# Keeping the residual by tokens, and writing the first FFN product of a transformer layer as seven block products

## The chip, the cores and the metric

The kernel runs on one core of a Trainium2 chip. The metric is the time of one execution in microseconds (us) on the device.

## The reference, cut to what matters

One layer with S = 512 tokens, D = 1024 features, an FFN width of 2816 and a side input p of width 256, all in float32:

```python
merged = sigmoid(gate_a) * (y_nsa @ w_up_nsa) + sigmoid(gate_b) * (y_moba @ w_up_moba)
x = x + merged @ w_out
gate, up = split(rms_norm(x, g_ffn) @ w_ffn_in, 2, axis=-1)
x = x + (silu(gate) * up) @ w_ffn_out
ple_gate = sigmoid(rms_norm(x, g_ple) @ w_ple_gate)
x = x + ple_gate * (p @ w_ple_proj)
```

`y_nsa` and `y_moba` come from two attention mixers (compressed, selected and windowed heads; block-selected heads), which the change leaves as they are.

## The kernel before, in words

**Precision and weights.** Each float32 matrix is split into a high half of reduced width and a low rest, and each product is three matmuls (high by high, high by low, low by high; helper `tmm`, L370 to L375). The class `Weights` (L57 to L104) keeps a list of units in the order of use. SyncE loads a unit of 128 x 1024 (512 KB) into `wr` (3 buffers), ScalarE copies the high half (`wh`, L87), VectorE subtracts the low half (`wl`, L88), 4 buffers each. `get` splits two units ahead and loads six ahead. The statements are put into each engine's order by the framework's scheduler, which reorders the program; each engine then works its own list in order and waits on semaphores.

**Stages.** Input projections and rotary embedding (0 to 160 us), attention (160 to 378) with the gate and up products woven in, the second up product, the output projection, the first FFN product (448 to 678), the second (678 to 788), the side input and its gate.

**Weight sums.** The second FFN product is done by blocks: the matrix is cut in 2 x 2 blocks, and seven half-size products replace eight (L1048 to L1089), four of them with sums of weight blocks. Those sums (`fs1` to `fs4`) are made in DRAM by `weight_sums` (L911 to L923): 32 transfers of 704 KB on GpSimd's software queue, 16 plain copies and 16 that accumulate, each issued after a mark that GpSimd copies once per attention step.

**Output projection** (L950 to L974). The residual `X2` is kept by features: eight tiles of 128 features x 512 tokens, from `xT`. Per tile, 24 matmuls with the weight stationary and 512 tokens moving; then `residual` adds the projection to `X2` on VectorE, `norm_split` writes the two halves of the tile times the gain (ScalarE L240, VectorE), and `add_square` sums the squares (ScalarE L250, GpSimd L251). The norm's factor is not in these halves.

**First FFN product** (L1007 to L1035). For each of 22 tiles `m`, a gate bank `fg` and an up bank `fu`, 24 matmuls of 512 columns each. After the first 48 matmuls `rms_stats` (L333 to L351) turns the sums of squares into the norm's factor with two small sets of TensorE matmuls (`st1b`, `st1c`), and spreads it to all partitions as `rb1`. Then VectorE multiplies by `rb1`, ScalarE takes the tanh, and GpSimd writes the product of gate and up to `HB` (L1033).

**Second FFN product** (`product`, L1048 to L1062). Each of the seven products has 132 matmuls of 256 columns with the weights stationary; between them VectorE and ScalarE combine and split the next operands (`prepare`), and VectorE adds the banks to `X2` (`add_to`). `row_done` splits the finished rows.

**Side input** (L1093 to L1125): load `pin`, product `pj`, statistics `st2`, then eight tiles of the gate product `pg` with 24 matmuls each; the output leaves by features.

## Time and profile before

| what | us |
|---|---|
| runs | 849.66, 852.53, 852.66 |
| median | 852.53 |
| the profiled execution's own time | 853.71 |
| its span in the trace | 851.9 |

The profile comes from one execution. PE is TensorE's matmuls, PEld its weight loads, DVE VectorE, ACT ScalarE, POOL GpSimd, SP SyncE, which issues the loads. A row of the stage windows gives, for a stretch of time, the busy time of each engine with its number of instructions, the clock granted to TensorE (1.00 is full), the share in which the DMA engines were busy, and their rate. A row of a chain or a timeline begins with the start and the duration in us. A group's row ends with the busy time and the mean ns of one instruction, then the idle time before the group. `q1` is the queue of SyncE's loads, `q0` GpSimd's software queue.

### The profile page before, as it was taken

The page shows a single profiled execution, that of the slowest core. Times are in us where ns is not written, and L with a number is a line of the kernel's source. Part 1 is how long each engine was busy: PE and PEld are TensorE (multiplying, and loading weights), DVE is VectorE, ACT ScalarE, POOL GpSimd, SP SyncE. Part 2 cuts the span into 40 slices and gives each one's busy share as a digit, 9 for nine tenths or more (in the row PEclk, how much of TensorE's full clock was granted, in tenths as well). Part 3 has the DMA queues.
Part 4 walks back from the last instruction along what each step waited for, and adds up shares of the span by engine and source line. Part 5 has one row for each costly group of instructions (what it writes and reads, how often), then busy time and mean ns, then how long its engine had stood idle before and what let it go on. Part 6 is the DMA issues. An engine that isn't in the chain of part 4 may idle for free.

```text
span 851.9 us, 12039 instructions
## 1 busy us (share of the span) xinstructions
PE 835.4 (98%) x4513; PEld 721.3 (85%) x4513; DVE 572.8 (67%) x989; ACT 412.0 (48%) x726; POOL 195.1 (23%) x239
## 2 busy tenths in 40 slices
PE   9979999999999999999999999999999999999997
PEld 7869898788788888788888888888888899999886
DVE  6797767888877988749536545454545599758563
ACT  7434655876667767634433222222222347436531
POOL 3764426000001212215322222222221200003100
PEclk9989999999999999999999999999999999999999
DMA  9414554224544668985322333323223265665321
GB/s 331 154 63 131 164 139 128 95 66 128 190 152 152 223 150 189 231 204 197 125 75 99 99 98 100 99 99 98 93 89 94 84 185 151 200 200 181 124 75 50
DMA packets 34282, 117.22 MB, mean 138 GB/s; under 512 B 4400, under 2 KB 4784, under 8 KB 34224
## 3 DMA queue, kind: packets, MB, share of 16 engines
q1 hardware_dynamic: 28688, 91.27, 33.1%
q0 software_dynamic: 4608, 23.07, 10.8%
q10 hardware_dynamic: 928, 2.11, 1.0%
q8 instruction: 35, 0.57, 0.3%
q14 instruction: 23, 0.19, 0.1%
HBM read 111.20 MB, written 25.17 MB: 160 GB/s over the span
## 4 chain that ended last, share of the span: by engine, by line
PE 90%; DVE 7%; ACT 2%; issue 1%; DMA 0%; POOL 0%; SPq 0%; DVEq 0%; ACTq 0%
PE fs L1061 7%; PE fg L373 5%; PE fu L373 5%; PE fg L375 5%; PE fu L375 5%; PE fg L374 5%; PE fu L374 5%; PE fa L1061 4%; PE ga L373 3%; PE pt L795 3%; PE ga L374 3%; PE ga L375 3%; DVE wl L88 2%; PE fv L1061 2%; PE pv L819 2%; PE pgb L375 2%
## 5 line engine op out<-in xcount | busy, mean ns | idle before, releaser
L87 ACT ACTIVATE wh<-wr 128x1024 fp32r<-128x1024 f32 (+2 forms) x163 | 164.6, 1014 | 291.8 <-PE fg L374 79.1
L88 DVE TENSOR_TENSOR wl<-wr,wh 128x1024 fp32r<-128x1024 f32 (+2 forms) x163 | 205.8, 1268 | 62.8 <-ACT wh L87 61.1
L1033 POOL TENSOR_TENSOR H<-zg,u 128x256 f32<-128x256 f32 x44 | 51.8, 1197 | 178.3 <-DVE u L1027 164.7
L373 PE MATMUL fg<-x2h,wh 128*128 128x512 f32 x176 | 68.6, 390 | 0.0
L373 PE MATMUL fu<-x2h,wh 128*128 128x512 f32 x176 | 68.6, 389 | 0.0
L375 PE MATMUL fg<-x2h,wl 128*128 128x512 f32 x176 | 68.5, 389 | 0.0
L374 PE MATMUL fu<-x2l,wh 128*128 128x512 f32 x176 | 68.5, 389 | 0.0
L374 PE MATMUL fg<-x2l,wh 128*128 128x512 f32 x176 | 68.5, 389 | 0.0
L375 PE MATMUL fu<-x2h,wl 128*128 128x512 f32 x176 | 68.5, 389 | 0.0
L373 PE MATMUL ga<-xh,wh 128*128 128x512 f32 x128 | 53.8, 420 | 0.0
L251 POOL TENSOR_TENSOR ssum<-ssum,sqx 128x512 f32<-128x512 f32 x14 | 23.5, 1680 | 131.3 <-ACT sqx L250 131.1
L770 DVE CUSTOM_DVE_ANT_0 p<-sb,big_mask 128x512 f32<-128x512 f32 (+2 forms) x96 | 44.8, 485 | 9.5 <-PE sb L768 7.8
L1027 DVE SCALAR_TENSOR_TENSOR u<-fu,rb 128x512 f32<-128x512 f32 x22 | 15.2, 691 | 52.7 <-PE fu L375 52.7
L374 PE MATMUL ga<-xl,wh 128*128 128x512 f32 x128 | 50.5, 394 | 0.0
L375 PE MATMUL ga<-xh,wl 128*128 128x512 f32 x128 | 50.4, 395 | 0.0
L1025 DVE TENSOR_TENSOR zg<-fg,rb 128x512 f32<-128x512 f32 x22 | 15.2, 691 | 49.9 <-PE fg L375 49.8
L795 PE MATMUL pt<-ident,p 128*128 128x128 f32 x240 | 38.6, 275 | 1.6 <-DVE pw L805 1.3
L375 PEld LDWEIGHTS fu<-x2h,wl 128*128 128x128 f32 x176 | 33.1, 188 | 7.0
L374 PEld LDWEIGHTS fg<-x2l,wh 128*128 128x128 f32 x176 | 33.1, 188 | 6.8
L373 PEld LDWEIGHTS fg<-x2h,wh 128*128 128x128 f32 x176 | 33.0, 188 | 6.8
L375 PEld LDWEIGHTS fg<-x2h,wl 128*128 128x128 f32 x176 | 33.0, 187 | 6.9
L374 PEld LDWEIGHTS fu<-x2l,wh 128*128 128x128 f32 x176 | 33.0, 187 | 6.8
(667 smaller groups left out, 2309.7 us busy)
## 6 DMA issues: line engine op xcount, KB each, us to landing
wr<-fi SPq DMA_DIRECT2D x44, 512.0 KB, 3.4
fs<-f POOLq DMA_DIRECT2D x24, 704.0 KB, 6.1
wr<-fs SPq DMA_DIRECT2D x20, 512.0 KB, 3.6
wr<-ga SPq DMA_DIRECT2D x16, 512.0 KB, 3.5
wr<-f SPq DMA_DIRECT2D x15, 512.0 KB, 3.6
fs<-fs POOLq DMA_DIRECT2D x8, 704.0 KB, 11.2
wr<-wo SPq DMA_DIRECT2D x8, 512.0 KB, 5.0
wr<-pg SPq DMA_DIRECT2D x8, 512.0 KB, 3.5
```

Of the source, the lines that this page charges most:

```text
L87: self.nc.scalar.activation(h[:, a:b], t[:, a:b], AF.Copy)
L88: self.nc.vector.tensor_sub(l[:, a:b], t[:, a:b], h[:, a:b].bitcast(F32))
L251: G.tensor_tensor(ssum, ssum, q, op=OP.add)
L373: T.matmul(o, wh[:, sl], h, start=start, stop=False)
L374: T.matmul(o, wh[:, sl], l, start=False, stop=False)
L375: T.matmul(o, wl[:, sl], h, start=False, stop=stop)
L770: V.tensor_tensor_reduce(out=p, in0=o, in1=big_mask[:, 512 - n:512], op0=OP.add, op1=OP.min, scale=1.0, scalar=3.0e38, accum_out=st["m"][: ...
L795: last = T.transpose(b[:, off:off + 128], st["p"][:, P_OFF[qt] + kb * 128:P_OFF[qt] + kb * 128 + 128], ident)
L819: T.matmul(o, job["v"](kb), st.pop(("pl", kb))[:, cols], start=False, stop=job["last"] and kb == 2)
L1025: V.tensor_tensor(zg, bg, rb1, op=OP.mult)
L1033: G.tensor_tensor(HB[f"{r + 1}{c + 1}"][j][:, k * 256:(k + 1) * 256], zg[:, t], u[:, t], op=OP.mult)
L1061: T.matmul(c, x, y, start=b.name not in seen, stop=kt == HF - 1 and i == 2, skip_group_check=True)
```

## The change

**Residual by tokens.** `X2` is now four tiles of 128 tokens x 1024 features, from `xN`. The output projection holds the activations stationary and moves 512 columns of weights; the last two of eight weight rows are taken token tile by token tile. `normed` then takes two token tiles at a time: Square with a running sum on ScalarE, a small step on VectorE, the power on GpSimd, and a scaled copy on ScalarE. `turned_x` turns the result by TensorE, four 128 x 128 blocks per bank of two banks, and ScalarE copies the banks to `B` (by features, one tile per half of the features and half of the tokens). `rms_stats` is no longer called for the two later norms.

**First FFN product by blocks.** The weights are cut in 2 x 2 blocks `g11` to `g22`, the activations likewise, and for each of 11 steps `p` seven products (`g11`, `s1`, `s2`, `g12`, `s3`, `s4`, `g22`) of 24 matmuls with 256 columns each are made. Two sums of weights, `gs1` and `gs3`, are made in DRAM during attention by `in_sums` (24 transfers, most of 1 MB, half of them accumulating, 23 MB as before). Two more, `s2` and `s4`, are added by VectorE per step from loaded tiles that are kept. The product of the two halves is now made by VectorE.

**The old weight sums** (`out_sums`, the same 32 transfers) are now issued in steps 0 to 7 of the first FFN product, four after each step's mark on GpSimd.

**Second FFN product and side input.** The activations are stationary, 512 weight columns move: 66 matmuls per product. The side input's product is done between the two transposes at the start of the FFN, goes to DRAM and is loaded back. The last norm uses `normed` and `turned_x` as well, one half of the tokens behind the sixth product, the other behind the first half of the gate product. The output leaves by tokens.

```diff
+        key, src, n, how = self.unit(i)
+        if src is None:
+            t, more = (self.kept.pop(k) for k in how["sum"])
+            self.nc.vector.tensor_tensor(t[:, :n], t[:, :n], more[:, :n], op=OP.add)
+        else:
+            t = self.raw.pop(i)
+        if how.get("keep"):
+            self.kept[key] = t
+        h, l = how["tiles"](i) if "tiles" in how else self.half_tiles(i)
         self.done[i] = (h, l)
...
+    for p in range(NP):
+        for nm, src in (("g11", a["g11"]), ("s1", gs["gs1"]), ("s2", ("s1", "g11")), ("g12", a["g12"]),
+                        ("s3", gs["gs3"]), ("s4", ("s2", "g12")), ("g22", a["g22"])):
+            if isinstance(src, tuple):
+                units.append(((nm, p), None, 1024, dict(sum=[(k, p) for k in src], keep=nm == "s2")))
+            else:
+                units.append(((nm, p), src[:, p * 1024:(p + 1) * 1024], 1024, dict(keep=nm in ("g11", "s1", "g12"))))
...
+    def transfer(dst, src, **kw):
+        with tc.issue_after(marks[-1]):
+            G.dma_start(dst, src, **kw)
+    def in_sums():
+        for c0, c1 in I_SUMS:
+            c = slice(c0, c1)
+            for dst in ("gs1", "gs3"):
+                transfer(gs[dst][:, c], a["g21"][:, c])
                 yield
-        for dst, base in (("fs1", "f21"), ("fs3", "f21"), ("fs2", "f11"), ("fs4", "f12")):
-            yield from parts(dst, base)
-        for dst, more in (("fs1", "f22"), ("fs3", "f11"), ("fs2", "fs1"), ("fs4", "fs2")):
-            yield from parts(dst, more, accum_op=OP.add)
+            for dst, more in (("gs1", "g22"), ("gs3", "g11")):
+                transfer(gs[dst][:, c], a[more][:, c], accum_op=OP.add)
+                yield
+    def out_sums():
+        parts = [slice(i * HF * 128, (i + 1) * HF * 128) for i in range(4)]
+        for dst, base in (("fs1", "f21"), ("fs2", "f11"), ("fs3", "f21"), ("fs4", "f12")):
+            for c in parts:
+                transfer(fs[dst][:, c], a[base][:, c])
+                yield
+        for dst, more in (("fs1", "f22"), ("fs2", "fs1"), ("fs3", "f11"), ("fs4", "fs2")):
+            for c in parts:
+                transfer(fs[dst][:, c], (fs[more] if more in fs else a[more])[:, c], accum_op=OP.add)
+                yield
 
...
-    run(weave(weave(weave(att, fill, *FILL_RATE), side, 0.2), delay(weight_sums(), 8), 0.2))
+    run(weave(weave(weave(att, fill, *FILL_RATE), side, 0.2), delay(in_sums(), 6), 0.2))
...
-    def residual(o, b, scale, gi):
-        t = X2[o]
-        V.scalar_tensor_tensor(t, b, scale, t, op0=OP.mult, op1=OP.add)
-        norm_split(t, gv[:, gi, o:o + 1], xh[o], xl[o])
-        add_square(t, o == 0)
...
+    X2 = [flat(t4(f"X2{tt}", F32)) for tt in range(QT)]
+    for tt in range(QT):
+        nc.sync.dma_start(X2[tt], a["xN"][tt])
+    seen = set()
+    def mm(o, b, sth, stl, mh, ml, stop):
+        T.matmul(o, sth, mh, start=b.name not in seen, stop=False, skip_group_check=True)
+        seen.add(b.name)
+        T.matmul(o, sth, ml, start=False, stop=False, skip_group_check=True)
+        T.matmul(o, stl, mh, start=False, stop=stop, skip_group_check=True)
+    def normed(c, name):
+        ss, rn = (small(f"{nm}_", [128, 2]) for nm in ("xs", "xr"))
+        xs = [flat(t4(f"{name}{tt}", F32)) for tt in (2 * c, 2 * c + 1)]
+        for i in range(2):
+            A.activation(xs[i], X2[2 * c + i], AF.Square, accum_out=ss[:, i:i + 1])
+        V.tensor_scalar(ss, ss, 1.0 / D, EPS, op0=OP.mult, op1=OP.add)
+        G.tensor_tensor(rn, ss, half_neg[:, :2], op=OP.pow)
+        for i in range(2):
+            A.activation(xs[i], X2[2 * c + i], AF.Copy, scale=rn[:, i:i + 1])
+        return xs
+    def turned_x(xs, tag, put):
+        for u in range(4):
+            b = bank("tx", tag)
+            for j in range(2):
+                for i in range(2):
+                    T.transpose(b[:, j * 256 + i * 128:j * 256 + i * 128 + 128],
+                                xs[i][:, (2 * u + j) * 128:(2 * u + j) * 128 + 128], ident)
+            for j in range(2):
+                put(2 * u + j, b[:, j * 256:j * 256 + 256])
...
+    def wo_part(n, u, w, tt):
+        for j in range(2):
+            kt = 2 * u + j
+            mh, ml = (x[:, j * 512:(j + 1) * 512] for x in w)
+            mm(wob[n][tt], wob[n][tt], MH[kt][:, tts(tt)], ML[kt][:, tts(tt)], mh, ml, kt == 7)
...
+    def split_x(nm, src):
+        h, l = op[nm] = [flat(t4(f"x{nm}{x}")) for x in "hl"]
+        A.activation(h, src, AF.Copy)
+        V.tensor_sub(l, src, h.bitcast(F32))
+    def put_b(c):
+        def put(kt, src):
+            A.activation(B[kt // 4][c][:, kt % 4 * 256:kt % 4 * 256 + 256], src, AF.Copy, scale=gv[:, 1, kt:kt + 1])
+        return put
...
+    for tt in range(QT):
+        for n in range(2):
+            wo_part(n, 3, w3[n], tt)
...
+        for n in range(2):
+            x = X2[tt][:, n * 512:(n + 1) * 512]
+            V.scalar_tensor_tensor(x, wob[n][tt], 0.5, x, op0=OP.mult, op1=OP.add)
+        if tt % 2:
+            xs[tt // 2] = normed(tt // 2, "xs")
+    turned_x(xs[0], "b", put_b(0))
+    split_x("11", B[0][0])
+    split_x("21", B[1][0])
...
+    def pj_part(n):
+        w = W.get(("pj", n))
+        for tt in range(QT):
+            b = bank("pjb", "va"[tt % 2])
+            for kt in range(2):
+                mh, ml = (x[:, kt * 512:(kt + 1) * 512] for x in w)
+                mm(b, b, PIh[:, kt, tts(tt)], PIl[:, kt, tts(tt)], mh, ml, kt == 1)
+            t = t2("pps")
+            A.activation(t, b, AF.Copy)
+            nc.sync.dma_start(ppd[tt][:, n * 512:(n + 1) * 512], t)
+    pj_part(0)
+    pj_part(1)
+    turned_x(xs[1], "b", put_b(1))
+    t1x, t2x = (flat(t4(f"x{nm}", F32)) for nm in ("t1", "t2"))
+    V.tensor_tensor(t1x, B[0][0], B[0][1], op=OP.subtract)
+    split_x("t1", t1x)
...
+    def in_product(key, p, b, nm):
+        w = W.get((key, p))
+        h, l = op[nm]
+        for q in range(2):
+            for kt in range(4):
+                wh, wl = (x[:, (q * 4 + kt) * 128:(q * 4 + kt) * 128 + 128] for x in w)
+                xh, xl = (x[:, kt * 256:kt * 256 + 256] for x in (h, l))
+                o = b[:, q * 256:q * 256 + 256]
+                T.matmul(o, wh, xh, start=b.name not in seen, stop=False, skip_group_check=True)
+                seen.add(b.name)
+                T.matmul(o, wh, xl, start=False, stop=False, skip_group_check=True)
+                T.matmul(o, wl, xh, start=False, stop=kt == 3, skip_group_check=True)
...
+    for p in range(NP):
+        X, Y, Z = bank("fx", "s"), bank("fy", "v"), bank("fz", "a")
+        in_product("g11", p, X, "11")
+        gl = copied(X, "gl")
+        in_product("s1", p, Z, "t1")
+        uh = copied(Z, "uh")
+        in_product("s2", p, X, "t2")
+        gh = copied(X, "gh")
+        in_product("g12", p, Y, "21")
+        gated(gl, Y)
+        in_product("s3", p, X, "t3")
+        V.tensor_tensor(uh, X, uh, op=OP.add)
+        in_product("s4", p, Z, "22")
+        gated(gh, Z)
+        put_h(2, p, gh, uh)
+        in_product("g22", p, X, "t4")
+        put_h(1, p, gl, X)
+        marks.append(G.tensor_copy(mark2[:, p:p + 1], gh[:, 0:1]).ins)
+        steps(sums, 4)
+        if p == 8:
+            split_op("f11", hb("11", 0))
...
+        for u in range(6):
+            w = W.get((nm, u))
+            if u and prepare:
+                prepare.pop(0)()
+            for j in range(2 if u < 5 else 1):
+                kt = 2 * u + j
+                mh, ml = (x[:, j * 512:(j + 1) * 512] for x in w)
+                for t in range(2):
+                    h, l = (x[:, kt % 4 * 256 + t * 128:kt % 4 * 256 + t * 128 + 128] for x in ops[nm][kt // 4])
+                    mm(banks[t], banks[t], h, l, mh, ml, kt == HF - 1)
...
+    x3 = normed(1, "x3s")
     product("f22", FX)
...
+    turned_x(x3, "b", put_x3(1))
+    add_to(1, 0, FX, 0.5)
...
+        if c == 1:
+            x3 = normed(0, "x3s")
+            turned_x(x3, "b", put_x3(0))
```

The first place is TensorE at the end of the output projection. `wob` is the projection's bank, `fg` and `fu` those of the first FFN tile, `x2h` and `x2l` the halves of the normed input. Before:

```order
L375 MATMUL wob<-MH_4195,wl_4438 128x512
L373 MATMUL fg<-x2h_4274,wh_4476 128x512 [waits DVE_49,Activation_49]
L374 MATMUL fg<-x2l_4275,wh_4476 128x512
L375 MATMUL fg<-x2h_4274,wl_4477 128x512 [waits DVE_49]
...
L373 MATMUL fg<-x2h_4393,wh_4476 128x512 [waits Activation_49]
L373 MATMUL fu<-x2h_4274,wh_4527 128x512
L337 MATMUL st1b<-ones,ssum 128x1 [waits Pool_49]
```

After, with `wo` the projection's banks, `xs` the scaled token tiles, `tx` the bank of a transpose, `fx` the first block product's bank, `x11h` and `x11l` the halves of its activations, `pjb` the side input's product:

```order
L1004 MATMUL wo_4216<-wh_4397,ML_4195 128x512
L1023 MATMUL tx<-ident,xs_4441 128x128 [waits DVE_49,Activation_49]
L1023 MATMUL tx<-ident,xs_4442 128x128 [waits Activation_49]
...
L1023 MATMUL tx<-ident,xs_4441 128x128 [waits PE_49,Activation_49]
...
L1023 MATMUL tx<-ident,xs_4479 128x128 [waits PE_49,Activation_49]
L1125 MATMUL fx<-x11h,wh_4575 128x256 [waits Activation_49]
L1127 MATMUL fx<-x11l,wh_4575 128x256 [waits DVE_49]
...
L1001 MATMUL pjb<-wh_4403,PIh 128x512 [waits Activation_49]
```

Before, the first FFN matmuls follow the projection at once and use the first tiles of the input; after, transposes stand between, the third and fourth bank of them behind a wait for ScalarE, and the side input's product behind the first block product.

The second place is ScalarE at the same point. Before, `X` is the residual, `sqx` its square, `wr` a loaded weight tile:

```order
L240 ACTIVATE x2h_4469<-X_4209,gv 128x512 [waits DMAHW3_49,DVE_49]
L250 ACTIVATE sqx<-X_4209 128x512 [waits Pool_49]
L87 ACTIVATE wh_4621<-wr_4441 128x1024 [waits DMAHW1_49,PE_49,Activation_49]
L240 ACTIVATE x2h_4469<-X_4209,gv 128x512 [waits DVE_49]
L250 ACTIVATE sqx<-X_4209 128x512 [waits Pool_49]
L87 ACTIVATE wh_4651<-wr_4480 128x1024 [waits DMAHW2_49,PE_49,Activation_49]
```

After, L1011 is the Square with its sum (`xs__` holds the sums), L1015 the scaled copy (`xr` is the factor), L1052 the copy from a bank to `B`:

```order
L1015 ACTIVATE xs_4442<-X_4202,xr__4440 128x1024 [waits Activation_49]
L1011 ACTIVATE xs_4479,xs__4477<-X_4203 128x1024 [waits DMAHW4_49,DVE_49]
L108 ACTIVATE wh_4575<-wr_4371 128x1024 [waits PE_49]
L108 ACTIVATE wh_4679<-wr_4401 128x1024 [waits PE_49]
L1011 ACTIVATE xs_4480,xs__4477<-X_4204 128x1024 [waits DMAHW5_49,DVE_49]
L1052 ACTIVATE B_4407<-tx,gv 128x256 [waits PE_49]
...
L1015 ACTIVATE xs_4479<-X_4203,xr__4478 128x1024 [waits Pool_49]
L1015 ACTIVATE xs_4480<-X_4204,xr__4478 128x1024 [waits Activation_49]
L1052 ACTIVATE B_4409<-tx,gv 128x256 [waits PE_49]
...
L1047 ACTIVATE x11h<-B_4407 128x1024 [waits Activation_49]
```

The copies that free the transposes' banks stand behind two Squares and two weight copies, and the second pair's scaled copies stand between the first four of them and the next.

The third place is GpSimd's queue of weight sums. `fs_75` to `fs_78` are the four sums in DRAM, `mark` the copies that space them. Before, in attention:

```order
L849 COPY mark<-as__3270 128x1 [waits DVE_49,Activation_49]
L917 DMA fs_75<-f 128x1408 [waits DMASW1_49]
L849 COPY mark<-as__3353 128x1 [waits DVE_49,Activation_49]
L917 DMA fs_75<-f 128x1408 [waits DMASW2_49]
L917 DMA fs_75<-f 128x1408 [waits DMASW3_49]
L849 COPY mark<-as__3450 128x1 [waits DVE_49,Activation_49]
```

After, in the first FFN product:

```order
L1169 COPY mark_4675<-gh 128x1 [waits DVE_49]
L946 DMA fs_75<-f 128x1408 [waits DMASW0_49]
L946 DMA fs_75<-f 128x1408 [waits DMASW1_49]
L946 DMA fs_75<-f 128x1408 [waits DMASW2_49]
L946 DMA fs_75<-f 128x1408 [waits DMASW3_49]
L1169 COPY mark_4675<-gh 128x1 [waits DVE_49]
L946 DMA fs_76<-fs_75 128x1408 [waits DMASW4_49,DMASW0_49]
```

Where one or two transfers followed an attention step, four now follow a step of the FFN, beside the loads of that step's weights.

More of the change, by code (lines that the diff above doesn't have):

```diff
@@ L26 @@
 HF = NF // 2
-FQ = 4 * HF * 128
+FQ = HF * 512
+NP = NF // 2
+IQ = NP * 1024
+I_SUMS = [(i * 2048, min(IQ, (i + 1) * 2048)) for i in range(6)]
 F_ORDER = ("f11", "f12", "fs2", "fs1", "fs3", "fs4", "f22")
@@ L180, in hybrid_kernel @@
     fs = {nm: dp.tile([128, FQ], F32, name=nm) for nm in ("fs1", "fs2", "fs3", "fs4")}
+    gs = {nm: dp.tile([128, IQ], F32, name=nm) for nm in ("gs1", "gs3")}
+    ppd = [dp.tile([128, D], F32, name=f"ppd{i}") for i in range(QT)]
     def t4(name, dt=F32R):
@@ new lines, in hybrid_kernel, with first @@
+    for j in (1, 2):
+        split_op("f11", hb("11", j))
+    for j in range(3):
+        split_op("f12", hb("21", j))
+    run(sums)
+    T1, T2 = {}, {}
+    def first(j):
+        c = cols(j)
+        b11, b12, b22 = (hb(nm, j)[:, c] for nm in ("11", "12", "22"))
+        T1[j], T2[j] = (flat(t4(f"T{x}{j}", F32)) for x in "12")
+        V.tensor_tensor(T1[j][:, c], b11, b12, op=OP.subtract)
+        V.tensor_tensor(b12, b22, b12, op=OP.subtract)
+        V.scalar_tensor_tensor(T2[j][:, c], b11, -1.0, b12, op0=OP.mult, op1=OP.subtract)
+        split_op("fs2", T2[j])
@@ new lines, in add_to, with put_x3, put @@
+    def add_to(row, c, banks, scale):
+        for t in range(2):
+            x = X2[2 * c + t][:, row * 512:(row + 1) * 512]
+            V.scalar_tensor_tensor(x, banks[t], scale, x, op0=OP.mult, op1=OP.add)
+    X3h, X3l = ([[flat(t4(f"x3{x}{c}{k}")) for k in range(2)] for c in range(2)] for x in "hl")
+    def put_x3(c):
+        def put(kt, src):
+            s_ = slice(kt % 4 * 256, kt % 4 * 256 + 256)
+            h, l = X3h[c][kt // 4][:, s_], X3l[c][kt // 4][:, s_]
+            A.activation(h, src, AF.Copy, scale=gv[:, 2, kt:kt + 1])
+            V.scalar_tensor_tensor(l, src, gv[:, 2, kt:kt + 1], h.bitcast(F32), op0=OP.mult, op1=OP.subtract)
+        return put
```

269 lines of the change are left out of this document (115 added, 154 removed).

## The prediction

> **What bounds the kernel now.** I read the page's shares first, then the windows of the stages that the change touches, then the chain that ended last.
>
> ```profile
> PE 835.4 (98%) x4513; PEld 721.3 (85%) x4513; DVE 572.8 (67%) x989; ACT 412.0 (48%) x726; POOL 195.1 (23%) x239
> ```
>
> ```profile
> core 0: us, PE busy (x) PEld busy (x) DVE busy (x) ACT busy (x) POOL busy (x), PEclk, DMA share, GB/s
> 160.00:378.00 218.00, 213.46 (x1175) 182.11 (x1174) 172.09 (x479) 152.44 (x355) 28.38 (x57) 0.99 0.62 168
> 448.00:678.00 230.00, 230.00 (x1023) 190.64 (x1023) 114.30 (x121) 61.77 (x70) 51.31 (x43) 1.00 0.30 98
> 678.00:788.00 110.00, 109.74 (x915) 109.53 (x914) 90.84 (x89) 60.76 (x70) 10.49 (x7) 1.00 0.57 178
> 809.00:852.00 43.00, 37.85 (x192) 32.06 (x190) 22.23 (x32) 9.54 (x14) 0.00 (x0) 0.98 0.17 62
> ```
>
> TensorE is the bound. The first FFN product (448 to 678) has it busy for the whole window at a granted clock of 1.00, with VectorE at half load and the DMA share at 0.30; the second one (678 to 788) idles 0.26 us in 110. So each matmul taken out there comes off the end, and each gap put in is added to it. The chain gives the prices of TensorE's other work:
>
> ```profile
> 325.30 0.87 PE pt L795 x8
> 447.47 0.79 PE st1b L337 x8
> 455.22 0.89 PE st1c L348 x8
> 677.81 15.83 PE fs L1061 x132
> 693.64 15.84 PE fv L1061 x132
> 796.32 0.79 PE st2b L337 x8
> 809.09 0.67 PE st2c L348 x6
> ```
>
> Eight transposes of 128x128 take 0.87 us (0.109 each); a product of 132 matmuls with 256 columns takes 15.84 us, so one steps by 0.1200 us. For 512 columns I take start to start from the timeline of TensorE in the output projection:
>
> ```profile
> 392.39 0.39 PE L373 MATMUL wob<-MH,wh 128*128 128x512 f32 x1
> 395.11 0.39 PE L373 MATMUL wob<-MH,wh 128*128 128x512 f32 x1
> ```
>
> These two are 12 matmuls apart: 2.72 / 12 = 0.2267 us each. Half the columns thus cost 53%, not 50%.
>
> **The change, part by part.** The sum is made against the profiled run's 853.71 us (span 851.9 and 1.8 around it), which lies 1.2 above the median of 852.53.
>
> TensorE's own work. First FFN product: 22 x 48 = 1056 matmuls of 512 columns are 239.4 us; now 11 x 7 x 24 = 1848 of 256 are 221.8: -17.6. Second: 7 x 132 = 924 of 256 are 110.9; now 7 x 66 = 462 of 512 are 104.7: -6.2. The statistics matmuls go: 0.79 + 0.89 and 0.79 + 0.67 (x6, so about 0.9 for 8): -3.4. Added are 64 transposes at 0.109: +7.0. Output projection, PLE gate and PLE projection keep their matmul counts (192, 192, 48 of 512 columns). Net -20.2.
>
> The Trainium skill, page "TensorE: Matmul & The Clock Gate", section "Back-to-back issue gap", gives N / 2.4 + 2.5 ns for a warm matmul, that is 109 ns and 216 ns here; by it the first term would be 1056 x 0.216 - 1848 x 0.109 = 26 us and not 17.6. The same section of the Trainium skill grants that this under-counts at small N, where the weight load is not in it. The rows above say 120.0 and 226.7, and the sum uses these.
>
> The entry to the first FFN product is where time is given back. Before, each feature tile of the residual was split as soon as its matmuls ended, and the norm's factor was only needed after the first 48 matmuls:
>
> ```profile
> 449.11 1.95 POOL L341 TENSOR_TENSOR st1rn<-ms__4592,half_neg 128x4 f32<-128x4 f32 x1 [8.25 <-DVE ms__4592 L339]
> 446.65 2.01 ACT L87 ACTIVATE wh<-wr 128x1024 fp32r<-128x1024 f32 x2 [7.73 <-issue]
> 688.74 1.21 DVE L88 TENSOR_TENSOR wl<-wr,wh 128x1024 fp32r<-128x1024 f32 x1
> 689.88 1.21 DVE L987 TENSOR_TENSOR fs2l<-T,fs2h 128x1024 fp32r<-128x1024 f32 x1
> L274 ACT ACTIVATE xn<-xn 128x1024 f32<-128x1024 f32 x4 | 4.2, 1057 | 0.4
> L804 ACT ACTIVATE phl<-pt 128x256 fp32r<-128x256 f32 x24 | 9.1, 378 | 9.3 <-PE pt L795 9.1
> ```
>
> Now the factor is applied before the transposes. From the end of tile 1's projection (t = 0): residual add on VectorE to 0.8; ScalarE's Square with its sum (1.06 + 0.19) to 2.05; VectorE's small step to 2.3; GpSimd's power (1.95) to 4.2; two scaled copies of 1.0 to 6.2. TensorE's last projection work, tiles 2 and 3 (24 x 0.2267), ends at 5.44. It turns eight blocks until 7.1 and then has no free bank: the copies out of the banks stand on ScalarE behind the second pair's two Squares and two weight copies (4 x about 1.1), so they start at 10.6 and the first four end at 12.3. The second pair's scaled copies take ScalarE to 14.8, the other four evacuations to 17.5 with the high half of the first operand (1.0) between them; VectorE's low half (1.14) ends near 17.9, and only then does the first block product run. Between 5.44 and 20.7 TensorE does 6.0 us of useful work: +9.3. The bounds are 6 (the copies go at the shorter step of 0.38 per 256 columns and nothing queues) and 13 (the PLE input, loaded behind a weight tile, comes late for the products that fill the gap).
>
> The clock follows such a gap. The trace has one of that length, and the windows after it:
>
> ```profile
> PE km L363 <- DVE kct L537: 3.1, 1, 3.1
> 51.60:55.00 3.40, 3.40 (x12) 2.83 (x11) 3.36 (x6) 0.48 (x2) 2.19 (x4) 0.50 0.45 152
> 65.20:72.00 6.80, 6.80 (x37) 5.82 (x36) 5.21 (x8) 4.96 (x8) 0.00 (x0) 1.00 0.42 104
> ```
>
> A wait of 3.1 us stands beside a stretch of 3.40 us at a granted clock of 0.50; such a stretch loses up to 1.7 us. One or two of them: +2 (0 to 5). The Trainium skill, same page, section "Part 1: The HAM clock gate", says that an idle window of about 3.4 us halves the clock until a busy one has passed; these rows agree with that (0.50, then 1.00).
>
> Inside the first FFN product VectorE gets nine 1024-wide passes per block of seven products (seven low halves and two weight sums) and seven 512-wide ones: 9 x 1.135 (688.74 to 689.88) + 7 x 0.60 = 14.4 us beside 168 x 0.12 = 20.2 of TensorE. It stays below; the product of the two halves moves off GpSimd, which had slowed VectorE:
>
> ```profile
> L88 DVE TENSOR_TENSOR wl<-wr,wh 128x1024 fp32r<-128x1024 f32 x43 | 61.4, 1427 | 18.5 <-ACT wh L87 18.5
> ```
>
> 1.427 there against 1.21 alone. I charge +0.5 for the first block, whose operands are still being combined.
>
> The DMA is the term I know least. The 32 transfers that sum the second product's weights move from attention into blocks 0 to 7 of this product, four per block, beside five loads per block. The rows of attention price both:
>
> ```profile
> q0 software_dynamic: 1321, 6.63, 38.2%
> q0 software_dynamic: 1354, 6.75, 87.4%
> q1 hardware_dynamic: 762, 2.33, 16.7%
> fs<-fs POOLq DMA_DIRECT2D x8, 704.0 KB, 11.2
> wr<-fi SPq DMA_DIRECT2D x10, 512.0 KB, 3.4
> pin<-pT SPq DMA_DIRECT2D x1, 512.0 KB, 12.7
> wr<-wo SPq DMA_DIRECT2D x1, 512.0 KB, 16.4
> 352.90 0.39 SPq L1094 DMA_DIRECT2D pin<-pT  x1
> 354.00 40.27 SPq L70 DMA_DIRECT2D wr<-wo  x6
> ```
>
> Plain copies (250 to 300) cost 38.2% of 50 us for 6.63 MB, 2.9 us per MB, 2.1 per transfer; accumulating ones (340 to 378) 87.4% of 38 for 6.75 MB, 4.9 per MB, 3.55 per transfer. A load costs 16.7% of 38 x 0.524 / 2.33 = 1.4. Blocks 0 to 3 hold 4 x 2.1 + 5 x 1.4 = 15.4 us of transfers in 20.2: no stall. Blocks 4 to 7 hold 4 x 3.55 + 7 = 21.2, just over. If the engines serve both queues to the full, that is 4 us, nearly all inside the lead of about 3.6 us that the three buffers of each kind give: 0. If they take turns packet by packet, a load passes once per accumulation, 3.55 + 1.4 = 5.0 us, and the row pair 365.6 to 370.4 (issue plus time to landing) says 4.8; then the lead is used up in a block or two and three or four blocks end 2 to 4 us late: up to +16. I take +5, nearer to the shared case since four accumulations a block leave a rest.
>
> The second FFN product prepares its operands in shorter products (14.96 against 15.84 us) with VectorE at 15 to 16 of them: +0.5 (0 to 3). Behind it the first normed pair is turned while the second follows only after the first two gate tiles: its chain of Square, power and scaled copy is the 6 us of above, beside 21.8 us of matmuls; what shows is the wait for the copies: +2.2 (0 to 4). The tail loses one of VectorE's three steps behind the last matmul (0.43 us): -0.4. The weight sums for the first product take the place of the old ones in attention, 23 MB each way, on the same queue: 0 (-2 to 2).
>
> Sum: -20.2 + 9.3 + 2 + 0.5 + 5 + 0.5 + 2.2 - 0.4 = -1.1. From 853.71 that is 852.6, and on the median 851.4.
>
> **The rivals.** (1) Half the stall and shared transfers: the entry costs 5 and no half clock, the DMA 1. That takes 4.3 + 2 + 4 = 10.3 off: 841. For it: the scheduler interleaves the PLE products, and the loads of the 448 to 678 window land in 3.4 us. Against: the copies' place on ScalarE is fixed in the order. (2) On the slower side: the sums starve the loads. At 4.8 to 5.4 us per load, five loads need 24 to 27 us where a block has 20.2; over four blocks that is 15 to 27 less 3.6 of lead, say +18 in place of 5: 864. It decides where the load of a block's second weight tile, asked for about 10 us into the block before, lands more than 12 us later; the rows 12.7 and 16.4 are over that, the 11.2 of an accumulation itself just under. Against: these stood beside eight accumulations in a row, here they come in fours. (3) The step at 256 columns comes down to half of that at 512, 0.1133, so that the block products save all that their halved columns promise: 1848 x 0.0067 = 12.4 us more, 839. Against it stand two products of 132 matmuls at 0.120 in this very trace, which have the same shape. The Trainium skill's formula above leans this way, by 8.5 us in all.
>
> **How the numbers follow.** My own case has 0.50, with a range of 846 to 857 from the entry (6 to 13) and the DMA (0 to 10); rival 1 has 0.25, rival 2 0.22, rival 3 0.03. 0.5%, about what a measurement of this kernel can tell from no change, is 4.3 us: faster lies under 848.3, slower over 856.8. Of my own case some 0.08 falls under and 0.02 over, so faster 0.36, same 0.40, slower 0.24. The range from 840 to 863 takes in rival 1 and the lower half of rival 2; the rest of rival 2, rival 3 and what no term covers are left out.
>
> **What would show it.** Right: a first FFN product whose steady blocks take 20.2 us with TensorE full, a second one of about 105 us, and between the projection and the first block some 9 us of TensorE waiting for ScalarE (the transposes' banks), followed by windows at a clock of 0.50. The DMA term shows as TensorE waiting for weights in blocks 5 to 9 alone, with a DMA share near 1 there. Wrong: loads landing in under 5 us throughout (rival 1), blocks of 24 us (rival 2), matmul steps away from 120 and 227 ns, or VectorE waited for inside the steady blocks.

## The result, and the profile after

The changed kernel takes 845.32 us (median of 10 runs, 840.97 to 850.13), the kernel before 851.62 in as many runs beside it (849.49 to 853.35): a ratio of 0.9929, with a 95% interval of 0.9905 to 0.9953. It is faster by 0.7%, 6.3 us. The forecast had 851.4, most likely no change. Its range of 840 to 863 holds the result; the narrower range of its own case, 846 to 857, misses it by 0.7 us, on the side of the first rival (841). The profiled execution took 845.66 us. The page of its profile, and the stages that answer to those shown of before (the hole between projection and first steady block is a window of its own):

```profile
span 843.9 us, 12960 instructions
PE 818.0 (97%) x4875; PEld 725.1 (86%) x4875; DVE 620.5 (74%) x1049; ACT 478.4 (57%) x823; POOL 144.9 (17%) x218
```

```profile
160.00:378.00 218.00, 213.55 (x1180) 182.25 (x1179) 171.11 (x478) 151.44 (x352) 23.97 (x50) 1.00 0.64 174
432.60:460.00 27.40, 21.37 (x108) 17.96 (x107) 16.05 (x15) 21.93 (x38) 1.66 (x1) 0.81 0.30 103
460.00:640.00 180.00, 180.00 (x1500) 179.74 (x1499) 137.45 (x149) 92.72 (x112) 26.68 (x41) 1.00 0.85 257
680.00:788.00 108.00, 107.42 (x485) 88.93 (x484) 83.86 (x87) 58.18 (x64) 1.42 (x2) 1.00 0.63 191
797.00:843.00 46.00, 42.37 (x217) 35.90 (x215) 20.79 (x33) 16.32 (x28) 0.70 (x1) 0.99 0.26 92
```

TensorE's busy time has gone from 835.4 to 818.0 us and it is still the bound: 180.00 of 180 in the steady blocks, at a clock of 1.00, with VectorE at 137 and the DMA engines at 0.85. What it gave back stands in the second row, and in its waits from the output projection to the end (engine, line and what was waited for; then us in total, times, longest):

```profile
PE tx L1023 <- ACT B L1052: 5.7, 3, 3.2
PE pgb L1001 <- ACT wh L108: 1.9, 1, 1.9
PE fx L1125 <- ACT gl L1132: 1.7, 1, 1.7
PE fa L1003 <- DVE wl L109: 0.6, 1, 0.6
PE pgb L1003 <- DVE wl L109: 0.5, 1, 0.5
PE pgb L1001 <- ACT pz L1267: 0.5, 1, 0.5
PE tx L1023 <- DVE X L1061: 0.3, 1, 0.3
```

The first row and the last are the entry: the transposes wait for ScalarE to free their banks, and once for VectorE's residual add. The rows of `pgb` are the gate product behind the second FFN product; the kernel before has waits of 0.4 (`wl`) and 0.5 (`pz`) there, and one of 0.3 before `fa`. The wait of `fx` for `gl`, the copy by which ScalarE frees that bank, ends at 646.5 us, in block 9 of the first FFN product (blocks and steps are counted from 0 to 10).

### The profile page after: what moved, and what is told of

Read it like the earlier page. It is cut to its first block, busy times and chain, and to the rows that moved or that the text cites. A ratio compares the mean times of both kernels' runs of the same rounds, so it can differ in the third digit from the quotient of the medians.

```text
span 843.9 us, 12960 instructions
## 1 busy us (share of the span) xinstructions
PE 818.0 (97%) x4875; PEld 725.1 (86%) x4875; DVE 620.5 (74%) x1049; ACT 478.4 (57%) x823; POOL 144.9 (17%) x218
## 5 line engine op out<-in xcount | busy, mean ns | idle before, releaser
L108 ACT ACTIVATE wh<-wr 128x1024 fp32r<-128x1024 f32 (+2 forms) x196 | 198.7, 1021 | 192.7 <-issue 32.2
L109 DVE TENSOR_TENSOR wl<-wr,wh 128x1024 fp32r<-128x1024 f32 (+2 forms) x196 | 233.1, 1199 | 97.3 <-ACT wh L108 96.9
L838 DVE TENSOR_TENSOR pw<-pt,pw 128x512 fp32r<-128x512 f32 x48 | 32.6, 682 | 7.0 <-ACT pw L837 6.9
L837 ACT ACTIVATE pw<-pt 128x512 fp32r<-128x512 f32 x48 | 28.1, 594 | 12.2 <-PE pt L828 11.8
L828 PEld LDWEIGHTS pt<-ident,p 128*128 128x128 f32 x240 | 28.9, 140 | 6.9 <-issue 1.4
L100 DVE TENSOR_TENSOR wr<-wr,wr 128x1024 f32<-128x1024 f32 x22 | 26.8, 1219 | 2.4 <-DMA wr<-g 2.3
L1001 PE MATMUL pgb<-wh,x3h 128*128 128x512 f32 (+1 forms) x72 | 25.9, 371 | 2.5 <-ACT wh L108 1.9
L1125 PE MATMUL fx<-xt2h,wh 128*128 128x256 f32 x88 | 25.8, 293 | 1.7 <-ACT gl L1132 1.7
L1003 PE MATMUL pgb<-wl,x3h 128*128 128x512 f32 (+1 forms) x72 | 26.1, 367 | 0.5 <-DVE wl L109 0.5
L1128 PE MATMUL fx<-xt2h,wl 128*128 128x256 f32 x88 | 25.6, 291 | 0.0
```

The source lines that it names most:

```text
L108: self.nc.scalar.activation(h[:, a:b], t[:, a:b], AF.Copy)
L109: self.nc.vector.tensor_sub(l[:, a:b], t[:, a:b], h[:, a:b].bitcast(F32))
L828: last = T.transpose(b[:, off:off + 128], st["p"][:, P_OFF[qt] + kb * 128:P_OFF[qt] + kb * 128 + 128], ident)
L1001: T.matmul(o, sth, mh, start=b.name not in seen, stop=False, skip_group_check=True)
L1003: T.matmul(o, sth, ml, start=False, stop=False, skip_group_check=True)
L1125: T.matmul(o, wh, xh, start=b.name not in seen, stop=False, skip_group_check=True)
```

## The experiments

All runs in one table, with the starts of three stages read from TensorE's timeline: the output projection, the first matmul of `fy` (taken as the end of the entry), and the gate product `pgb`. The last three columns are differences: entry (first to second start), FFN (second to third), rest (third to the end of the span). From the projection on, the two profiles of before both take 459.5 us. Each row's starts and span come from one profiled execution, its median from all runs. The first matmul of `fy` is a mark in the order, not always the end of the entry's work: in the combined kernels A and C the last eight transposes come behind it.

| kernel | median us (runs) | projection | `fy` | `pgb` | span | entry | FFN | rest |
|---|---|---|---|---|---|---|---|---|
| before | 851.62 (10) | 392.39 | | 789.04 | 851.9 | | | 62.9 |
| before, second look | 852.09 (1) | 390.76 | | 787.41 | 850.3 | | | 62.9 |
| changed | 845.32 (10) | 389.12 | 459.75 | 789.36 | 843.9 | 70.6 | 329.6 | 54.5 |
| changed, again | 843.78 (6) | 391.30 | 462.48 | 788.81 | 843.5 | 71.2 | 326.3 | 54.7 |
| no sums in the FFN | 844.57 (6) | 389.84 | 461.13 | 786.22 | 842.4 | 71.3 | 325.1 | 56.2 |
| three sums per step | 845.86 (6) | 388.62 | 459.14 | 786.11 | 842.3 | 70.5 | 327.0 | 56.2 |
| eight sums per step | 860.32 (4) | 389.21 | 460.59 | 802.48 | 858.7 | 71.4 | 341.9 | 56.2 |
| no sums in attention | 843.58 (4) | 388.22 | 459.52 | 784.76 | 840.9 | 71.3 | 325.2 | 56.1 |
| bank copies on VectorE | 843.78 (6) | 391.21 | 460.47 | 787.53 | 842.1 | 69.3 | 327.1 | 54.6 |
| side input first | 843.16 (4) | 390.26 | 455.96 | 787.16 | 841.8 | 65.7 | 331.2 | 54.6 |
| no norm factor | 843.01 (4) | 389.63 | 457.29 | 785.33 | 841.1 | 67.7 | 328.0 | 55.8 |
| combined A | 841.31 (6) | 389.55 | 450.96 | 783.95 | 838.9 | 61.4 | 333.0 | 55.0 |
| combined B | 845.68 (6) | 391.16 | 460.43 | 791.23 | 845.4 | 69.3 | 330.8 | 54.2 |
| combined C | 841.00 (5) | 391.08 | 452.50 | 786.31 | 842.3 | 61.4 | 333.8 | 56.0 |

The last column has two values, 54.2 to 55.0 and 55.8 to 56.2, and they don't follow the edits. They follow the clock at the gate product, in the same 20 us, in the changed kernel and in the one without sums in the FFN:

```profile
780.00:800.00 20.00, 17.47 (x83) 13.87 (x82) 10.55 (x16) 10.38 (x18) 0.24 (x1) 1.00 0.63 215
```

```profile
780.00:800.00 20.00, 17.48 (x77) 13.75 (x76) 8.63 (x14) 11.06 (x18) 0.70 (x1) 0.91 0.64 227
```

The waits are the same (1.9 and 0.5 us), but the second execution has a stretch of some 3.4 us at half clock behind them. All six profiles with 0.91 at this place have the higher value, all six with 1.00 the lower one. These 1.5 us come with the execution and not with the edit, so a single profile's time can't rank two edits this close.

### The weight sums beside the loads

Theory S: loads and sums share the DMA engines, which are busy to the full in steps 4 to 7; this uses up the lead of the weight buffers and ends in one late load. Theory R: the wait at 646 us comes from work that ScalarE gets in step 8. A third reading is the forecast's second rival, loads that starve. The profile of the changed kernel shows the load of `g` late on ScalarE between 635 and 655 us, and for 562 to 642 us the two queues and the loads' time to landing:

```profile
ACT wh L108 <- DMA wr<-g: 3.4, 1, 3.4
```

```profile
q0 software_dynamic: 2286, 11.44, 70.8%
q1 hardware_dynamic: 2802, 10.25, 32.7%
...
wr<-g SPq DMA_DIRECT2D x12, 512.0 KB, 13.0
...
wr<-gs SPq DMA_DIRECT2D x8, 512.0 KB, 11.2
```

**No sums in the first FFN product.**

```diff
-        src = fs[nm] if nm in fs else a[nm]
+        src = a[{"fs1": "f21", "fs2": "f11", "fs3": "f21", "fs4": "f12"}.get(nm, nm)]
-    sums = out_sums()
+    sums = iter(())
```

> Leaves out the 32 transfers that sum the second product's weights; the products load an unsummed block of the same size instead. Theory S (the sums share the DMA engines with the loads, use up the lead of the weight buffers in steps 4 to 7 and cost one late load at the end, 1.9 us): the wait of TensorE near 646 us goes, steps of 20.2 us throughout, 1 to 3 us less than the changed kernel (842 to 844). Rival R (the wait comes from the two splits that ScalarE gets in step 8): the wait stays, same time. The forecast's price: 5 us less.

Measured: 844.57 us, ratio to before 0.9925 (0.9907 to 0.9943). The wait near 646 us is gone. The same stretch of this run, 562 to 642 us:

```profile
wr<-g SPq DMA_DIRECT2D x12, 512.0 KB, 4.2
wr<-gs SPq DMA_DIRECT2D x8, 512.0 KB, 3.6
```

Each load lands in 4 us where it took 11 to 13 beside the sums, and still the medians differ by only 0.75 us (0.3 by the ratios), well within the intervals; theory S had 1 to 3 us. The loads are three times slower and TensorE hardly waits: the lead of the buffers hides most of it. The forecast's 5 us lie outside of what the two intervals allow (some 3 us).

**Three sums per step.**

```diff
-        steps(sums, 4)
+        steps(sums, 3)
```

> Three transfers per step over eleven steps in place of four over eight. Theory S: an accumulating step needs 3 x 3.3 + 5 x 1.4 = 17 us of the DMA engines in 20.2, so the lead is kept and the 1.9 us wait goes: about 843. Rival R: the wait stays, 845. If the end of the sums now reaches into the second product, its first loads of sums are late: up to 3 us more.

Measured: 845.86 us, 0.9938 (0.9917 to 0.9958). The wait in block 9 is gone, as S has it and R has not; one profile alone would not show that, but it is absent from all five with three sums per step or none, and present in five of the six with four. The 843 that S expected for the time is missed. In its place the second FFN product waits 1.0 us for the low half of a weight sum (before `fa`, at 733 us; 0.6 in the changed kernel). From the projection on it takes 453.7 us, between the 454.8 and 452.2 of the changed kernel's two profiles. No gain in the time.

**Eight sums per step.** The edit is `steps(sums, 8)` in the same place.

> Eight transfers per step over four steps: the DMA engines are asked for 8 x 3.3 + 7 = 33 us in two steps of 20.2. If the loads get what they ask for and the sums wait, no step grows and the time is 843 to 846. If both queues take turns packet by packet, 16 loads pass with 16 accumulations at 4.7 us each, 75 us where the steps give 65, less a lead of 3.6: 7 us more, 852. If the loads queue behind the sums (the forecast's second rival): 15 us more or worse, 860.

Measured: 860.32 us, 1.0103 (1.0086 to 1.0121), 15 us over the changed kernel. The steps in which the sums accumulate, in windows, and TensorE's waits between 500 and 610 us:

```profile
542.00:562.00 20.00, 17.63 (x145) 17.23 (x145) 12.06 (x13) 8.57 (x11) 4.25 (x6) 1.00 1.05 265
562.00:582.00 20.00, 15.87 (x116) 15.26 (x115) 12.79 (x13) 7.50 (x9) 3.26 (x4) 0.91 1.05 262
582.00:602.00 20.00, 16.30 (x117) 16.10 (x116) 11.88 (x15) 7.72 (x10) 1.45 (x3) 0.83 0.84 227
```

```profile
PE fx L1125 <- ACT gh L1132: 3.7, 1, 3.7
PE fy L1125 <- ACT wh L108: 2.3, 1, 2.3
PE fx L1128 <- DVE wl L109: 2.2, 2, 1.7
PE fz L1125 <- ACT wh L108: 1.7, 1, 1.7
PE fz L1128 <- DVE wl L109: 1.1, 2, 0.8
```

The second and third rows have 116 and 117 matmuls in 20 us where a step without a wait has 168 in 20.16, and in the second the DMA engines are at 1.05; the clock falls to 0.91 and 0.83 behind the waits. This is the forecast's second rival, seen at twice the dose: it is real, and four transfers per step stay mostly short of it. Of the three cases laid down, the one in which the loads queue behind the sums is the nearest (15 us); the turn-taking that I had priced at 7 is too mild by half.

**No sums in attention.**

```diff
-("s1", gs["gs1"])
+("s1", a["g21"])
-("s3", gs["gs3"])
+("s3", a["g21"])
-delay(in_sums(), 6)
+delay(iter(()), 6)
```

> Leaves out the 24 transfers that sum the first product's weights during attention; unsummed blocks of the same size are loaded. Theory: TensorE is full in attention and its loads are in time with or without the sums, so the output projection starts at 389 as in the changed kernel, within 1.5 us, and the time is the same. Rival: the sums cost attention 2 to 4 us, which the changed kernel saved in part by spreading them in larger pieces; then it starts 2 us or more earlier, 842 to 843.

Measured: 843.58 us, 0.9915 (0.9891 to 0.9939). The projection starts at 388.2, 0.9 us earlier than in the changed kernel and less than the spread of these starts. Attention pays nothing that can be seen for the sums. The wait in block 9 does not appear in this profile although the sums of that stage are all there: its size differs from one execution to the next. In the other profiles with four sums per step it is 1.1 (changed, again), 0.4 (copies on VectorE), 0.8 (side input first) and 1.5 with 0.8 one block earlier (no factor).

### The part that did not change

The changed kernel's profile starts its projection 3.3 us before the first profile of before, on the same instructions of TensorE and VectorE.

> The kernel before, unchanged, for a second profile. In the first one the output projection starts at 392.4 us, in five profiles with the changed code at 388.2 to 389.8, though the instructions ahead of it are the same but for the sums' transfers. Theory H (the first profile was a slow draw of that part): it starts at 388 to 390.5 here. Rival (the change made attention faster by some 3 us): it starts at 391.5 to 393 again.

Measured: 390.76, in the gap between the two expectations. Other runs help: the kernel with the bank copies on VectorE, which is the changed one up to the entry, has 391.21, and the changed kernel's second profile 391.30.

Over all profiles the start lies between 388.2 and 391.3 with the changed code and at 390.8 and 392.4 with the old. The ranges overlap, so the 3.3 us can't be put down to the change; that a small part of them belongs to it isn't excluded. The comparison of stages is therefore made from the projection on: 459.5 twice before, 454.8 and 452.2 after, 4.7 to 7.3 us less.

### The entry

Theory E: TensorE waits because the copies out of the transposes' banks stand in ScalarE's list behind two Squares and two weight copies. Theory N: the way through the norm sets the entry, whoever copies. ScalarE's timeline in the changed kernel, from the end of the projection at 432.6:

```profile
432.45 1.04 ACT L1011 ACTIVATE xs<-X 128x1024 f32<-128x1024 f32 x1
...
433.49 1.99 ACT L108 ACTIVATE wh<-wr 128x1024 fp32r<-128x1024 f32 x2
435.38 1.04 ACT L1011 ACTIVATE xs<-X 128x1024 f32<-128x1024 f32 x1
...
436.54 1.57 ACT L1052 ACTIVATE B<-tx,gv 128x256 f32<-128x256 f32 x4
438.77 2.19 ACT L1015 ACTIVATE xs<-X,xr__4478 128x1024 f32<-128x1024 f32 x2 [0.67 <-POOL xr__4478 L1013]
```

This is the order of the forecast's walk, and the same windows show the clock:

```profile
434.00:438.00 4.00, 0.81 (x6) 0.57 (x4) 3.44 (x4) 3.98 (x8) 0.92 (x1) 0.76 0.01 2
438.00:442.00 4.00, 1.66 (x8) 1.25 (x7) 0.18 (x1) 3.33 (x6) 0.74 (x1) 0.50 0.65 201
442.00:446.00 4.00, 3.85 (x17) 3.33 (x17) 2.75 (x3) 3.36 (x5) 0.00 (x0) 0.50 0.18 65
446.00:450.00 4.00, 4.00 (x26) 3.64 (x25) 1.72 (x2) 1.98 (x4) 0.00 (x0) 0.96 0.00 0
```

ScalarE works 3.98 of 4 us while TensorE works 0.81, and some 10 us pass at half clock: by the shares of the first and the last row, from about 436.1 to 446.3.

**Bank copies on VectorE** (the first pair's only).

```diff
+            if c == 0:
+                V.tensor_scalar(o, src, gv[:, 1, kt:kt + 1], None, op0=OP.mult)
+            else:
+                A.activation(o, src, AF.Copy, scale=gv[:, 1, kt:kt + 1])
```

> The eight copies out of the first pair's transposes go to VectorE in place of ScalarE. Theory E (TensorE waits at the entry because these copies stand in ScalarE's list behind two Squares and two weight copies, as the forecast's working has it): the first copy starts 3 us earlier, the first block product 3 to 5 us earlier, the time falls by 2 to 4 us from the changed kernel's, to 841 to 843. Rival N (the way through the norm of both pairs sets the entry, whoever copies): the wait only moves, 844 to 846.

Measured: 843.78 us, 0.9911 (0.9894 to 0.9927). TensorE's waits between 430 and 475 us in this run:

```profile
PE fx L1131 <- DVE x11l L1048: 2.4, 1, 2.4
PE fx L1129 <- ACT x11h L1047: 1.6, 1, 1.6
PE tx L1023 <- DVE B L1054: 0.4, 2, 0.2
PE tx L1023 <- DVE X L1065: 0.3, 1, 0.3
```

The banks are waited for 0.4 us in place of 5.7, and the first block product starts 4.9 us behind the first transpose in place of 10.0, as E says. But its operands are then waited for, 2.4 and 1.6 us, and the entry as a whole is 1.4 to 1.9 us shorter. The time equals the second set of runs of the changed kernel (843.78), 0.2 under the 844 to 846 of N and above the 841 to 843 of E. The place of the wait was E's; the sum was nearer to N's.

**Side input first.**

```diff
+    pin = t4("pin", F32)
+    nc.sync.dma_start(pin, a["pT"].rearrange("k p t -> p k t"))
...
+    A.activation(PIh, pin, AF.Copy)
+    V.tensor_sub(PIl, pin, PIh.bitcast(F32))
     xs = [None, None]
...
+    pj_part(0)
     turned_x(xs[0], "b", put_b(0))
...
-    pj_part(0)
     pj_part(1)
```

> The side input is loaded and split before the residual, and half of its product (24 matmuls of 512 columns, 5.4 us) stands ahead of the first transposes, the other half right behind the first eight. Theory E: the hole of 27.1 us with 17.3 us of work takes in 10.9 us of ready work where the waits are; waits of TensorE there fall from 6 us to under 2, the stretch at half clock goes too, 4 to 8 us less: 837 to 841. Rival N: the second pair's way through ScalarE, now without the side input's matmuls to cover it, opens a hole behind the transposes of the same size: 844 to 847.

Measured: 843.16 us, 0.9908 (0.9895 to 0.9921). Waits between 430 and 475 us:

```profile
PE tx L1023 <- ACT B L1052: 2.4, 2, 2.1
PE fz L1127 <- DVE xt1l L1048: 1.7, 1, 1.7
PE fx L1127 <- DVE xt2l L1048: 1.4, 1, 1.4
PE fx L1125 <- ACT x11h L1047: 0.3, 1, 0.3
```

The entry is 4.9 to 5.5 us shorter, but the FFN stage is 1.6 to 4.9 longer: the combined operands `xt1` and `xt2` are now late on VectorE, which the side input's matmuls had covered. Both expected times are missed, E's 837 to 841 and N's 844 to 847; N named a new hole, and it came at another place and about half the size. The time is not clear of the changed kernel's.

**No norm factor.**

```diff
-            A.activation(xs[i], X2[2 * c + i], AF.Copy, scale=rn[:, i:i + 1])
+            A.activation(xs[i], X2[2 * c + i], AF.Copy, scale=0.5)
```

> Leaves the norm's factor out ahead of the first product and of the gate (a constant stands in its place; sums and powers are still computed). Theory E: the scaled copies no longer wait for GpSimd, but the bank copies still stand behind the same work on ScalarE: 1 to 2 us less, 843 to 844. Rival N: the chain through GpSimd is what holds the entry: 4 us less or more, 841 or under.

Measured: 843.01 us, 0.9897 (0.9872 to 0.9922). The time is the 843 that E expected, though not clear of the changed kernel's 845.32 and 843.78. In the profile the entry is 3.0 to 3.5 us shorter with no wait for GpSimd left. The wait for the banks is still 3.0 us of the former 5.7. So by these profiles the norm's chain through GpSimd is about a third of the 9.8 us that the entry loses. That the rest is ScalarE's and VectorE's work, and the half clock behind it, is argued from the waits and not shown by an edit of its own.

### Put together

**Combined A and B.** A takes the copies on VectorE, the side input first, three sums per step, and `W.depth = 5` ahead of the seventh block product; B leaves the side input where the change has it.

> Three edits together: the first pair's bank copies on VectorE, the side input's product ahead of and between the transposes, three weight sums per step over eleven steps; and the splits of the last weights five units ahead from the seventh block product on. Theory E and S: the entry's lost time falls from 9.8 us to under 4, the 1.9 us wait at the sums goes, the 2.8 us wait for weights at the gate product goes: 837 to 840. Rival N (behind the earlier start VectorE's splits of the combined operands are late, as in the run with the side input first): the two edits of the entry give no more than one of them, 842.

> As the run before, but with the side input's product left where the change has it. Theory: the gain of the copies on VectorE (1.5 in the times, 3.9 in the trace from the projection on) plus up to 1.9 at the sums plus up to 2.8 at the gate product: 838 to 841. Rival: the wait at the gate product is for the turned input and not for the weights; then 842 to 843.

> The changed kernel itself on the same chip as the two runs before, for their comparison: 845.3 within 1.5, with the first wait at the transposes of 3.2 us and a wait near step 9 of 0 to 1.9 us.

Measured: A 841.31 us, 0.9902 (0.9878 to 0.9926); B 845.68, 0.9940 (0.9925 to 0.9956); the changed kernel on the same chip 843.78, 0.9911 (0.9895 to 0.9928). The changed kernel's 843.78 is at the lower edge of what was expected for it, with the wait of 3.2 us at the transposes and 1.1 in block 9. A's entry takes 61.4 us. The projection's 43.5 us (389.12 to 432.64 in the changed kernel) and the 16.4 us of work that A has behind it and ahead of `fy` (17.3 less eight transposes) make 59.9, so 1.5 us are lost there in place of 9.8, and no half clock is left:

```profile
432.00:440.00 8.00, 8.00 (x41) 6.73 (x40) 5.76 (x9) 7.43 (x11) 1.66 (x1) 1.00 0.18 68
440.00:448.00 8.00, 7.09 (x40) 5.70 (x38) 5.91 (x11) 7.30 (x11) 0.00 (x0) 1.00 0.73 254
448.00:456.00 8.00, 7.14 (x56) 6.74 (x56) 6.62 (x8) 6.83 (x13) 0.00 (x0) 1.00 0.40 131
456.00:464.00 8.00, 5.51 (x43) 5.31 (x44) 8.00 (x8) 5.33 (x6) 0.00 (x0) 1.00 0.23 74
```

VectorE is at 8.00 of 8 in the last row, and TensorE at 5.51: behind the first `fy` TensorE waits 3.6 us for split operands (1.7 for `xt1l`, 1.4 for `xt2l`). So part of the lost time has moved behind `fy`, and the FFN stage is 3.4 to 6.7 us longer than the changed kernel's. From the projection on A takes 449.3 us, 2.9 to 5.4 less than the changed kernel's two profiles. Its 841.31 lies above the 837 to 840 of E and S, nearest to N's 842. At the gate product the edit turned the wait for weights into one for the turned input. Its waits there, between 780 and 800 us, in A and then in B:

```profile
PE pgb L1001 <- ACT x3h L1230: 2.6, 2, 1.9
```

```profile
PE pgb L1001 <- ACT x3h L1230: 4.6, 2, 3.1
```

The wait that B's rival named is thus there, but B's 845.68 is above the rival's 842 to 843 too. ScalarE has both the splits and the turned input to do, and whichever comes second is late. A and B differ by the place of the side input alone, on one chip, and their intervals touch only at the edge (0.9926 and 0.9925): the 4.4 us between them are the clearest sign that the side input's place counts once the copies are on VectorE.

**Combined C** is A without that edit.

> The first of the two combined kernels without its edit at the gate product (the splits five units ahead). If that edit gave nothing (its waits of 0.7 and 1.9 us for the turned input took the place of 1.9 and 0.5 us for weights), the time is the same, 840 to 842, and the waits for weights at the gate product are back. If it cost time, as in the second combined kernel, where they were 3.1 and 1.5 us: 1 to 2 us less, 839 to 840.

Measured: 841.00 us, 0.9877 (0.9861 to 0.9893), the fastest of all, on another chip than A. The waits for weights at the gate product are back (1.9 and 0.5 us). In A the edit thus gave nothing that can be seen; from the projection on C's profile also has two stretches at half clock that A's has not, so the two profiles do not rank it. C's interval lies below that of the changed kernel's second set of runs (0.9895 to 0.9928) by little; A's does not.

## Why the prediction was right or wrong, point by point

- **TensorE's own work, -20.2.** Right. GpSimd's marks stand one per step, here those of steps 7, 8 and 9:

```profile
619.02 0.70 POOL L1169 COPY mark<-gh 128x1 f32<-128x1 f32 x1 [10.41 <-DVE gh L1139]
639.18 0.71 POOL L1169 COPY mark<-gh 128x1 f32<-128x1 f32 x1 [10.54 <-DVE gh L1139]
662.80 0.71 POOL L1169 COPY mark<-gh 128x1 f32<-128x1 f32 x1 [22.92 <-DVE gh L1139]
```

  The first two are 20.16 us apart: for 168 matmuls that is 0.1200 each, the step of before. The third rival (0.1133) is ruled out by this. The Trainium skill's formula for an isolated matmul ("TensorE: Matmul & The Clock Gate", section "Back-to-back issue gap") gives 109 ns for 256 columns; the step measured here is longer, on the side to which that section says the formula errs at small N. The 8.5 us by which the formula was said to lean towards this rival "in all" are those of the first FFN product alone; with the second one, where it would save 1.2 us and not 6.2, an estimate by the same formula is 3.6.
- **The entry, +9.3, and the clock, +2.** The walk was right in the order of ScalarE's list and little more than a microsecond late: counted from the end of tile 1's projection, the copies out of the banks start at 9.3 us (forecast 10.6) and VectorE's low half ends at 16.7 (17.9). The hole from 432.64 to 459.75 holds 17.3 us of work (32 transposes, 24 and 48 matmuls), so 9.8 us are lost, clock included, against 11.3. Waits make 6.0 of it and not 9; the rest is work at half clock and the starts behind the waits. The half clock lasted 10.2 us, three stretches of the length that the forecast read from the trace of before and not one or two, and it came during the waits, over a time when TensorE had little to do.
- **The first block, +0.5.** No wait there: 0.
- **The DMA, +5.** This is the term that failed, in its size. In the changed kernel's profile step 9 takes 23.62 us (the last two marks above). The wait of 1.7 us is half of the excess; the other half is the clock, which stood at half for 3.4 us behind it (647.7 to 651.1) while TensorE was full:

```profile
640.00:660.00 20.00, 18.28 (x141) 18.07 (x140) 12.68 (x13) 10.00 (x12) 0.00 (x0) 0.91 0.50 158
```

  From the mark of step 1 to that of step 10 this profile takes 3.6 us more than nine steps of 20.16. The other five profiles with four sums per step take 0.2 to 2.7 more, so 1.8 on average; the one without sums 0.1 less. Both bounds of the forecast were real, next to 0 in one profile and 15 at twice the dose, and the step "I take +5" put the value between them by judgement. The queues' shares fit a small cost, though this is an argument: loads were 32.7% and sums 70.8%, together just over full, so in four steps little more than the lead goes. The forecast's point of decision, a landing later than 12 us, was also too strict: the median was 13.0 and 11.2 through four steps before TensorE waited.
- **The second FFN product, +0.5:** 0.6 (`fa` for `wl`) in this profile and no wait in the second one. **The gate product, +2.2:** 2.4, but for weights whose splits stand behind the copies, not for the copies themselves; in six of the twelve profiles with the changed code the clock adds some 1.5, which the forecast did not have.
- **The tail, -0.4.** Right: behind the last matmul stand one step of ScalarE and two of VectorE, where VectorE had three. From the last matmul's start to the end of the span it is 4.3 us (839.56 to 843.9) in place of 4.8 (847.09 to 851.9).
- **Attention, 0.** Nothing in the experiments speaks against it.

With the measured terms the forecast's sum is -20.2 + 9.8 + 0 + 3.6 + 0.6 + 2.4 - 0.4 = -4.2, and from the projection on this profile has -4.7 (the waits of 0.3 and 0.4 us that the kernel before has at the same places bring it to -4.9). For the second profile the terms are 10.4 for the entry, 1.3 for the DMA and 2.4 for the gate product: -6.5, against -7.3. The difference between "no change" and "faster" was mainly the DMA term, 1.4 to 3.7 us too dear in these two profiles, with the entry and its clock, 0.9 to 1.5 us too dear. The first rival had the DMA about right (1) and the entry wrong (5 and no half clock), and its sign, loads that land in under 5 us, did not come: they were late and it cost little. The second would have been right with twice the transfers per step.

## What to carry to other kernels

Where transfers move under a stage with weight loads, add up the time of both per step and compare it with the step. Here, over it by about as much as the buffers' lead, they cost 0.2 to 3.6 us though each load took three times as long; at twice the transfers per step they cost 15. A hole in the bound engine that comes from other engines' lists is not closed by moving its work about: each edit here removed the wait that it named and met the next one, and only a kernel with two of them together (C) came out clear of the changed kernel, by little. Count a wait with the clock behind it: the 1.7 us in block 9 cost 3.5. And a profile's stages that the change does not touch give the draw of the run; compare from where the code begins to differ.

## What the runs showed of the hardware that was not expected

A wait much shorter than the one of 3.1 us from which the prediction worked can bring the clock to half. In block 9 of the changed kernel TensorE waited for 1.7 us between matmuls, worked at full clock for 1.2 us more, and then ran at half clock for 3.4 us without any gap. At the gate product the same wait of 1.9 us is followed by such a stretch in six of the ten profiles that have it, and not in the other four. Read in windows of 0.5 us, every stretch at half clock in the 14 profiles is 3 to 3.5, 6.5 to 7 or 10 to 10.5 us long, except where the span ends: one, two or three times some 3.4. At the entry it is three in the changed kernel, two with the bank copies on VectorE or without the norm's factor, one with the side input first, none in A. That these lengths come from a fixed window in which the work is counted is a guess; no run here tests it.

At the entry the longest single wait was 3.2 us: waits of 3.2 and 2.3 us with transposes between them gave about 10 us at 0.50, and 3.85 us of work in the window of 442 to 446 us did not lift it at once. The Trainium skill ("TensorE: Matmul & The Clock Gate", section "Part 4: PE-mode transpose") says that transposes do not count as busy for the clock in the way that matmuls do. The rows of the entry would fit that but do not need it, since the clock also fell in block 9, where there are no transposes, and no run here separates the two.

Accumulating transfers on the software queue beside loads kept the DMA engines at a share of 1.03 to 1.05 with 252 to 275 GB/s, in the changed kernel and the eight-sum kernel. Plain copies beside loads, in an earlier step of the eight-sum kernel, gave 391 GB/s at 1.01:

```profile
502.00:522.00 20.00, 19.66 (x164) 19.45 (x163) 12.80 (x15) 8.58 (x11) 3.63 (x7) 1.00 1.01 391
```
